# Hybrid encoder block on one core: another order of the head blocks, other PSUM banks for the pooling products, and other start addresses for the out projection's operands

## The chip, the cores and the metric

The kernel runs as one program on one core of a Trainium2 chip. The metric is the device time of one execution in microseconds (us), as the median of several runs. The profiled execution is a separate one with its own time.

## What is computed

One layer of a hybrid encoder block on x of 256 tokens by 1024 channels, all in float32:

```
h = rmsnorm(x) * gain
z = h @ w_in        # 8192 columns: a_in 512 | a_gate 512 | q, k, v 1536 each | b_gate 512 | merge gates 2048
y_a = (per-group linear(multi-scale centred mean pooling(a_in) - a_in) * scale * silu(a_gate)) @ w_proj_a
att = dilated attention(q, k, v) with relative-position bias   # 3 dilation groups x 8 heads of 64
y_b = (att * silu(b_gate)) @ w_proj_b
merge = sigmoid(gA) * y_a + sigmoid(gB) * y_b
y = rmsnorm(x + merge @ w_out) * final_gain
```

## The kernel before

**Precision.** Each product is made of three matmuls in a rounded float32 format (`mm3`, lines 248 to 251). Both operands are split into a high part, a copy in that format (by ScalarE, line 129 for weights), and a low part, the remainder (by VectorE, line 134). The three are high by high, high by low and low by high, summed in PSUM. Every weight tile of 8 KB a partition is loaded by a DMA (line 112) into one of four raw buffers, and then cut into high and low parts, which have three buffers each. `cut_half` does half a tile, and a call of it follows nearly every accumulation tile, so that the cuts run a few tiles ahead of the matmuls.

**Tiles.** A projection tile (`project_t`, `project_v`) is an accumulation of 8 x 3 = 24 matmuls of 128 x 128 by 256 columns into one of three PSUM banks, tag "mm". In `project_t` the weights are stationary and the normalized input's parts `hh` and `hl` are moving; for v (`project_v`) it is the other way round. The other PSUM tags are "S" (one buffer of two banks, for the scores), "T" (two single banks, for transposes) and "O" (one bank, for the attention outputs).

**Order of the work.** The heads are done in two halves I = 0 and 1. The program runs through k, q and v of half 0, then six weight tiles for the pooling input u, its gate a and the attention gate b (two accumulation tiles for each weight tile), then v, k and q of half 1, then the eight weight tiles of the merge gates g (`gate_tile`, sixteen accumulation tiles), with the pooling products mx ahead of the last of them. Then follow the two branch projections y (`branch`: with the pooling branch's AMH and AML, then with the attention's ATHL), and last the out projection (`out_mm`, accumulators "both" and "out"), whose stationary operands are MH and ML, the parts of the merged result; its weights are moving.

**The head blocks.** A half has eight blocks (I, hq, b): four heads and two blocks b of 128 queries. A block has three stages. `stage_s` makes the scores with four matmuls into S (names sp), then VectorE adds the bias (lines 297 and 303, the latter with the row's extreme), ScalarE takes the exponential (306), VectorE divides by the sum (309 to 312). `stage_t` turns three 128 x 128 pieces with PE (line 318, pt) and splits them (320, 321). `stage_o` makes the value products (lines 332 and 335, op) into O, one half of the bank for each b, and after b = 1 the bank is read by ScalarE (346) and twice by VectorE (347, 348).

A small planner, `step()` (lines 355 to 372), puts these stages between accumulation tiles. It is called after each of them. Each call may do one value product, one transpose stage and one score stage, in this order. A transpose stage is due two calls after its scores (`LAG_T`), a value product two calls after the transposes (`LAG_O`). Scores start by a due time: every call with blocks waiting adds `rate`, and when `due` is over 0.99 the next block starts and 1 is taken off. The rate is 0.5 for half 0, where the blocks lie in u, a, b, and v of half 1, and 0.667 for half 1, where they lie in the merge gates. Lines 497 and 560 put the eight blocks of a half into the waiting list.

Outside the opening, the instructions of an engine are ordered by a scheduler which mostly follows the order of the program text; the waits between engines are generated. Buffers with one tag follow each other in turn. The keys are needed on the other 64 partitions too, and are copied there by DMAs from GpSimd's queue (line 442), one for even and one for odd heads of each dilation group.

**Addresses.** SBUF slots are laid out in the order in which their tags first appear. `skip(n, name)` reserves n bytes that nothing uses, so it moves the slots behind it. As built, these are the start addresses modulo 512 bytes: `hh` and `hl` 64, all high and low weight parts 128, AMH, AML and ATHL 64, MH and ML 192. Steps inside these tiles are multiples of 512 bytes. MH lies in the slot "bias", which holds the bias tables BT before, and ML in the slot "kl", 32 elements behind its start.

Of the kernel before, what the change touches and what calls it, by code (L numbers as in the profile page):

```python
# [12 lines left out]
F32R = mybir.dt.float32r  # L13
# [4 lines left out]
P = 128  # L18
D = 1024
S = 256  # L20
# [22 lines left out]
def encoder_block(ctx: ExitStack, tc: tile.TileContext, x, w_in, lines, w_pool, w_proj_a, w_proj_b,  # L43
# [9 lines left out]
    def slot(shape, dt, tag, name, bufs=1):  # L53
        return sb.tile(shape, dt, tag=tag, name=name, bufs=bufs)

    def skip(nbytes, name):

        if nbytes:
            sb.tile([P, nbytes // 4], F32, name=name)

    def bank(shape, tag, name, bufs):
        return ps.tile(shape, F32, tag=tag, name=name, bufs=bufs)

    def mmb(name, shape=(P, S)):
        return bank(list(shape), "mm", name, 3)
# [76 lines left out]
    def weights(n):  # L142
        return parts.pop(n)
# [28 lines left out]
    with tc.manual_schedule(engines={mybir.EngineType.Activation, mybir.EngineType.DVE, mybir.EngineType.PE,  # L172
# [35 lines left out]
        acc = bank([P, 2, 512], "S", "k00", 1)  # L208
# [39 lines left out]
    def mm3(acc, ah, al, bh, bl, first, last):  # L248
        nc.tensor.matmul(acc, ah, bh, start=first, stop=False)  # L249
        nc.tensor.matmul(acc, ah, bl, start=False, stop=False)  # L250
        nc.tensor.matmul(acc, al, bh, start=False, stop=last)  # L251
# [34 lines left out]
    def stage_s(I, hq, b):  # L286
        q = QS[I]
        bs = slice(b * P, (b + 1) * P)
        bl, bt = BL[I], BT[I]

        sp = bank([P, 2 * 512], "S", f"sp{I}{hq}{b}", 1)
        for g in (1, 2):
            o = sp[:, 0:512].rearrange("p (x c) -> p x c", x=2)[:, :, (g - 1) * P:g * P]
            nc.tensor.matmul(o, q[:, hq, g, bs], KX[I][:, hq, g - 1, b], start=True, stop=True)
        for x in range(2):
            nc.tensor.matmul(sp[:, 512:768], q[:, hq, 0, bs], K1[I][:, hq, x], start=x == 0, stop=x == 1)
        nc.vector.tensor_tensor(bl, sp[:, S:2 * S], bt[:, hq, 384:640], op=ALU.add)
        st = slot([P, 512], F32, "st", f"st{I}{hq}{b}", 3)
        nm = slot([P, 1], F32, "nm", f"nm{I}{hq}{b}", 3)
        bias_ = bass.AP(tensor=bl.tensor, offset=bl.offset,  # L300
                        ap=[list(bl.ap[0]), [S + hq * 640 + P * (1 - b), 2], [1, S]])
        scores = bass.AP(tensor=sp.tensor, offset=sp.offset, ap=[list(sp.ap[0]), [512, 2], [1, S]])
        nc.vector.tensor_tensor_reduce(st.rearrange("p (a c) -> p a c", c=256), scores, bias_, scale=-1.0,  # L303
                                       scalar=3.0e38, op0=ALU.add, op1=ALU.min, accum_out=nm)
        l = slot([P, 1], F32, "l", f"l{I}{hq}{b}", 3)
        e = nc.scalar.activation(st, st, AF.Exp, bias=nm, scale=-1.0, accum_out=l)  # L306
        behind(e, last_sig[0])

        nc.vector.tensor_tensor(st[:, P:S], st[:, P:S], st[:, 0:P], op=ALU.add)
        rl = slot([P, 1], F32, "rl", f"rl{I}{hq}{b}", 3)  # L310
        nc.vector.reciprocal(rl, l)
        nc.vector.tensor_scalar(st[:, P:], st[:, P:], rl, None, op0=ALU.mult)
        return st

    def stage_t(I, hq, b, st):
        tp = bank([P, 3, P], "T", f"pt{I}{hq}{b}", 2)
        for c in range(3):
            nc.tensor.transpose(tp[:, c, :], st[:, (c + 1) * P:(c + 2) * P], ident)
        pp = slot([P, 3, 2, P], F32R, "pp", f"pp{I}{hq}{b}", 2)
        nc.scalar.activation(pp[:, :, 0, :], tp, AF.Copy)  # L320
        nc.vector.tensor_tensor(pp[:, :, 1, :], tp, pp[:, :, 0, :].bitcast(F32), op=ALU.subtract)
        return pp
# [3 lines left out]
    def stage_o(I, hq, b, pp):  # L326
        if b == 0:
            opens[I, hq] = bank([P, 2, 2, P], "O", f"op{I}{hq}", 1)
        op = opens[I, hq]
        v = VS[I]  # L330
        for c in range(2):
            nc.tensor.matmul(op[:, b], v[:, c, hq], pp[:, 1 + c], start=c == 0, stop=False)
        for e in range(2):
            q = slice(e * 64, e * 64 + 64)
            nc.tensor.matmul(op[:, b, :, q], v[:, 2 + 2 * b + e, hq], pp[:, 0, :, q], start=False, stop=e == 1)
        if b == 1:
            h = I * 4 + hq
            rows = slice((h % 2) * 64, (h % 2) * 64 + 64)
            dst = ATT[rows, h // 2, :].rearrange("p (b r j) -> p b r j", b=2, r=2)

            def piece(lo, part):
                ap = op[lo * 64:lo * 64 + 64]
                return bass.AP(tensor=ap.tensor, offset=ap.offset + part * P + 63,
                               ap=[list(ap.ap[0]), [2 * P, 2], [64, 2], [-1, 64]])

            last_exp[0] = nc.scalar.activation(dst, piece(0, 0), AF.Copy)
            nc.vector.tensor_tensor(dst, dst, piece(0, 1), op=ALU.add)
            nc.vector.tensor_tensor(dst, dst, piece(1, 0), op=ALU.add)
# [4 lines left out]
    due, rate = [1.0 - RATES[0]], [RATES[0]]  # L353

    def step():
        clock[0] += 1
        for it in live:
            if it["at"] == "t" and it["when"] <= clock[0]:
                stage_o(*it["it"], it["p"])
                it["at"] = "done"  # L360
                break
        live[:] = [it for it in live if it["at"] != "done"]
        for it in live:
            if it["at"] == "s" and it["when"] <= clock[0]:
                it["p"] = stage_t(*it["it"], it["st"])
                it["at"], it["when"] = "t", clock[0] + LAG_O
                break
        due[0] = due[0] + rate[0] if wait else due[0]
        if wait and due[0] > 0.99:
            due[0] -= 1.0  # L370
            it = wait.pop(0)
            live.append({"it": it, "at": "s", "when": clock[0] + LAG_T, "st": stage_s(*it)})
# [95 lines left out]
    def bias(I):  # L468
        T = skew.pop(I)
        t = slot([P, S + 4 * 640], F32, "bias", f"BT{I}")  # L470
        BL[I], BT[I] = t[:, 0:S], t[:, S:].rearrange("p (h c) -> p h c", c=640)
        by = T.rearrange("p c a h -> p h a c")
        for h in range(4):
            nc.gpsimd.tensor_copy(BT[I][:, h, 0:384].rearrange("p (a c) -> p a c", c=64), by[:, h, 0:6])
        for rl in range(2):
            rows = slice(rl * 64, (rl + 1) * 64)
            for g in range(2):
                o = 384 + g * P + 64 * (rl if g == 0 else 1 - rl)
                nc.gpsimd.tensor_copy(BT[I][rows, :, o:o + 64], by[rows, :, 6 + g + rl])
                o = 384 + g * P + 64 * (1 - rl if g == 0 else rl)  # L480
                behind(nc.gpsimd.memset(BT[I][rows, :, o:o + 64], MASK), first_lo)
# [6 lines left out]
    heads(0, "k")  # L488

    heads(0, "q")  # L490
    bias(0)
    U = sb.tile([P, 4, UW], F32, tag="uu", name="U")
    nc.gpsimd.memset(U[:, :, 0:PAD], 0.0)
    nc.gpsimd.memset(U[:, :, PAD + S:], 0.0)
    heads(0, "v")
    skip(608, "pt")
    wait += [(0, hq, b) for hq in range(4) for b in range(2)]


    for dst in ("u", "a", "b"):  # L500
        for t in range(2):
            hi, lo = weights(n)
            for u in range(2):
                acc = project_t(hi, lo, u, f"{dst}{t}{u}")
                g = 2 * t + u
# [50 lines left out]
    heads(1, "q")  # L556
    bias(1)
    rate[0] = RATES[1]
    due[0] = 1.0 - rate[0]
    wait += [(1, hq, b) for hq in range(4) for b in range(2)]  # L560


# [25 lines left out]
    PH, PL = PHL[:, 0], PHL[:, 1]  # L588
# [6 lines left out]
    AML = slot([P, 4, S], F32R, "t4", "AML")  # L595
    wph, wpl = weights(n)
    n += 1
    for g in range(4):
        acc = mmb(f"mx{g}") if g < 3 else bank([P, 2, 512], "S", "mx3", 1)[:, 0, 0:S]
        mm3(acc, wph[:, g, :], wpl[:, g, :], PH[:, g, :], PL[:, g, :], True, True)  # L600
        am = AM[:, g, :].rearrange("p (r j) -> p r j", r=4)
        nc.vector.scalar_tensor_tensor(am, acc.rearrange("p (j r) -> p r j", r=4), prm[:, 24 + g:25 + g],
                                       SA[:, g, :].rearrange("p (r j) -> p r j", r=4), op0=ALU.mult,
                                       op1=ALU.mult)
# [47 lines left out]
    squash((GG[:, 8:12], G2))  # L652

    MH = slot([P, 8, S], F32R, "bias", "MH")
    ML = slot([P, 8 * S + 32], F32R, "kl", "ML")[:, 32:].rearrange("p (c j) -> p c j", j=S)

    def done_b(cb, acc):
        nc.vector.tensor_tensor(GB[cb], acc, GB[cb], op=ALU.mult)
        nc.gpsimd.tensor_tensor(GA[:, cb, :], GA[:, cb, :], GB[cb], op=ALU.add)
        nc.scalar.activation(MH[:, cb, :], GA[:, cb, :], AF.Copy)  # L660
        nc.vector.tensor_tensor(ML[:, cb, :], GA[:, cb, :], MH[:, cb, :].bitcast(F32), op=ALU.subtract)

# [22 lines left out]
    def out_mm(kh, nh, tb):  # L685
        hi, lo = wo[kh, nh]
        c = slice(tb * P, (tb + 1) * P)
        for i in range(2):
# [4 lines left out]
            for k in range(4):  # L693
                kc = kh * 4 + k
                mm3(acc, MH[:, kc, c], ML[:, kc, c], hi[:, k, cs], lo[:, k, cs], kc == 0, kc == KC - 1)

# [145 lines left out]
```

## Time and profile before

| | |
|---|---|
| median of 3 runs | 260.26 us (259.99 to 260.36) |
| profiled execution | 260.05 us, span 258.3 us |
| mean granted TensorE clock | 0.993 |
| matmuls / weight loads | 2160 / 2160 |
| DMA | 52.01 MB in 9992 packets |

The page of the profile lists the engines' busy time, the chain of work that ended last, and the costliest groups of instructions by line. The timeline lists instructions by start and length, with the idle time of the engine before them and what ended it. The windows view sums each engine's busy time in a stretch; there "(x147)" counts the instructions that touch the stretch. Durations of matmuls overlap, since the next one starts before the last has left the array, so the distance between starts, not the duration, is what one costs. PE stands for the matmuls, PEld for the weight loads, DVE for VectorE, ACT for ScalarE, POOL for GpSimd.

### The profile page before, as it was taken

Reading aid. Unit: us, or ns where it says so; the run is one execution under the profiler, and the core shown is the slowest. Engines: PE = TensorE matmul, PEld = TensorE weight load, DVE = VectorE, ACT = ScalarE, POOL = GpSimd, SP = SyncE. Lnnn points to the kernel's source line nnn. Section 1 sums busy time; section 2 is a strip of 40 time slices with the busy share of each in tenths; the row PEclk is TensorE's granted clock in tenths of the full one; section 3 lists DMA queues with packets and bytes.
Section 4 is the critical chain, followed back from the end, with each engine's and each line's share of the span. In section 5 each row is a group of like instructions: output and inputs, shape, how many; then the busy total and the mean of one; then the engine's idle time right before and its main releaser. Section 6 shows DMA issues by size and latency. Waiting matters only on the chain.

```text
span 258.3 us, 5483 instructions
## 1 busy us (share of the span) xinstructions
PE 250.5 (97%) x2160; PEld 249.1 (96%) x2160; DVE 209.4 (81%) x408; ACT 164.6 (64%) x286; POOL 76.6 (30%) x105
## 2 busy tenths in 40 slices
PE   8999999999999999999999999999999999999990
PEld 8899999999999999999999999999999999999990
DVE  2899979778888787889697997967849998899383
ACT  4878577565666565658967778655549994446140
POOL 1562419201798000010671950000210030442011
PEclk9999999999999999999999999999999999999997
DMA  6998999996444644454899897144440598300022
GB/s 232 385 414 325 275 258 326 302 323 241 166 162 162 246 162 166 162 165 162 261 259 210 287 249 302 46 165 162 160 167 0 179 371 291 141 3 1 3 81 81
DMA packets 9992, 52.01 MB, mean 201 GB/s; under 512 B 1147, under 2 KB 2142, under 8 KB 4718
## 3 DMA queue, kind: packets, MB, share of 16 engines
q1 hardware_dynamic: 7022, 44.08, 49.6%
q0 software_dynamic: 2512, 7.12, 11.2%
q10 hardware_dynamic: 432, 0.46, 0.5%
q8 instruction: 17, 0.28, 0.4%
q14 instruction: 9, 0.07, 0.1%
HBM read 47.42 MB, written 1.09 MB: 188 GB/s over the span
## 4 chain that ended last, share of the span: by engine, by line
PE 86%; DVE 6%; issue 3%; DMA 2%; ACT 1%; POOLq 0%; POOL 0%; SPq 0%; DVEq 0%; ACTq 0%
PE v L249 4%; PE v L251 4%; PE v L250 4%; PE q L251 4%; PE q L249 4%; PE q L250 4%; PE g L249 4%; PE g L251 4%; PE g L250 4%; PE k L249 4%; PE k L251 4%; PE k L250 4%; PE y L249 3%; PE y L251 3%; PE y L250 3%
## 5 line engine op out<-in xcount | busy, mean ns | idle before, releaser
L134 DVE TENSOR_TENSOR wlo<-wraw,whi 128x512 fp32r<-128x512 f32 (+1 forms) x130 | 107.5, 865 | 8.3 <-ACT whi L129 7.4
L129 ACT ACTIVATE whi<-wraw 128x1024 fp32r<-128x1024 f32 (+1 forms) x80 | 81.0, 1038 | 22.7 <-PE q L250 10.1
L249 PE MATMUL g<-hh,whi 128*128 128x256 f32 x128 | 35.8, 279 | 0.0
L251 PE MATMUL g<-hh,wlo 128*128 128x256 f32 x128 | 35.4, 276 | 0.0
L250 PE MATMUL g<-hl,whi 128*128 128x256 f32 x128 | 35.3, 276 | 0.0
L306 ACT ACTIVATE st<-st,nm 128x512 f32<-128x512 f32 x16 | 11.6, 724 | 28.7 <-DVE nm L303 28.7
L249 PE MATMUL v<-whi,hh 128*128 128x256 f32 x96 | 26.6, 277 | 0.0
L251 PE MATMUL v<-whi,hl 128*128 128x256 f32 x96 | 26.5, 276 | 0.0
L250 PE MATMUL v<-wlo,hh 128*128 128x256 f32 x96 | 26.5, 276 | 0.0
L251 PE MATMUL q<-hh,wlo 128*128 128x256 f32 x96 | 26.5, 276 | 0.0
L249 PE MATMUL q<-hh,whi 128*128 128x256 f32 x96 | 26.5, 276 | 0.0
L250 PE MATMUL q<-hl,whi 128*128 128x256 f32 x96 | 26.5, 276 | 0.0
L249 PEld LDWEIGHTS g<-hh,whi 128*128 128x128 f32 x128 | 24.0, 188 | 0.1
L250 PEld LDWEIGHTS g<-hl,whi 128*128 128x128 f32 x128 | 24.0, 188 | 0.0
L251 PEld LDWEIGHTS g<-hh,wlo 128*128 128x128 f32 x128 | 24.0, 188 | 0.0
L249 PE MATMUL k<-hh,whi 128*128 128x256 f32 x80 | 22.2, 277 | 0.0
L251 PE MATMUL k<-hh,wlo 128*128 128x256 f32 x80 | 22.1, 277 | 0.0
L250 PE MATMUL k<-hl,whi 128*128 128x256 f32 x80 | 22.1, 277 | 0.0
L250 PEld LDWEIGHTS v<-wlo,hh 128*128 128x128 f32 x96 | 18.0, 188 | 0.0
L250 PEld LDWEIGHTS q<-hl,whi 128*128 128x128 f32 x96 | 18.0, 188 | 0.0
L251 PEld LDWEIGHTS q<-hh,wlo 128*128 128x128 f32 x96 | 18.0, 188 | 0.0
L249 PEld LDWEIGHTS q<-hh,whi 128*128 128x128 f32 x96 | 18.0, 188 | 0.0
(179 smaller groups left out, 764.1 us busy)
## 6 DMA issues: line engine op xcount, KB each, us to landing
wraw<-in_w_in_dram SPq DMA_DIRECT2D x31, 1024.0 KB, 6.6
wraw<-in_w_out_dram SPq DMA_DIRECT2D x4, 1024.0 KB, 5.6
T<-line_d POOLq DMA_DIRECT2D x4, 576.0 KB, 8.7
KX<-KX POOLq DMA_DIRECT2D x8, 256.0 KB, 17.2
wraw<-in_w_proj_a_dram SPq DMA_DIRECT2D x2, 1024.0 KB, 4.9
wraw<-in_w_proj_b_dram SPq DMA_DIRECT2D x2, 1024.0 KB, 4.9
X<-in_x_dram SPq DMA_DIRECT2D x2, 512.0 KB, 4.2
wraw<-in_w_in_dram SPq DMA_DIRECT2D x2, 512.0 KB, 6.6
```

Source lines behind the costliest of these rows:

```text
L129: nc.scalar.activation(hi[:, s, :], t[:, s, :], AF.Copy)
L134: (nc.gpsimd if kind == "pool" else nc.vector).tensor_tensor(lo[:, s, :], t[:, s, :], hi[:, s, :].bitcast(F32), op=ALU.subtract)
L249: nc.tensor.matmul(acc, ah, bh, start=first, stop=False)
L250: nc.tensor.matmul(acc, ah, bl, start=False, stop=False)
L251: nc.tensor.matmul(acc, al, bh, start=False, stop=last)
L306: e = nc.scalar.activation(st, st, AF.Exp, bias=nm, scale=-1.0, accum_out=l)
```

## The change

There are four edits, none of which changes a value that is computed.

1. A call of `step()` stands between v and u of half 0. The first block's scores come there, and all later stages of half 0 one accumulation tile earlier.
2. The due time at the start of half 1 is 2 x (1 - 0.667) = 0.666 in place of 0.333, so the blocks' scores follow other calls of `step()`.
3. The first two pooling products keep the "mm" banks and the third and fourth get the two banks of S; before, three had "mm" banks and the fourth the first bank of S. All twelve matmuls are written ahead of the four readings by VectorE.
4. Of the 608 bytes left empty behind the slot "bias", 384 are moved ahead of it, and ML starts at its slot's beginning. So MH moves by +384 bytes and ML by -128; both then start at 64 modulo 512. Slots further behind stay where they were.

```diff
--- before.py
+++ after.py
@@ -488,13 +488,16 @@
     heads(0, "k")
 
     heads(0, "q")
+    skip(384, "pb")
     bias(0)
     U = sb.tile([P, 4, UW], F32, tag="uu", name="U")
     nc.gpsimd.memset(U[:, :, 0:PAD], 0.0)
     nc.gpsimd.memset(U[:, :, PAD + S:], 0.0)
     heads(0, "v")
-    skip(608, "pt")
+    skip(224, "pt")
     wait += [(0, hq, b) for hq in range(4) for b in range(2)]
+
+    step()
 
 
     for dst in ("u", "a", "b"):
@@ -556,7 +559,8 @@
     heads(1, "q")
     bias(1)
     rate[0] = RATES[1]
-    due[0] = 1.0 - rate[0]
+
+    due[0] = 2.0 * (1.0 - rate[0])
     wait += [(1, hq, b) for hq in range(4) for b in range(2)]
 
 
@@ -595,9 +599,13 @@
     AML = slot([P, 4, S], F32R, "t4", "AML")
     wph, wpl = weights(n)
     n += 1
+
+    pair = bank([P, 2, 512], "S", "mx2", 1)
+    mx = [mmb("mx0"), mmb("mx1"), pair[:, 0, 0:S], pair[:, 1, 0:S]]
     for g in range(4):
-        acc = mmb(f"mx{g}") if g < 3 else bank([P, 2, 512], "S", "mx3", 1)[:, 0, 0:S]
-        mm3(acc, wph[:, g, :], wpl[:, g, :], PH[:, g, :], PL[:, g, :], True, True)
+        mm3(mx[g], wph[:, g, :], wpl[:, g, :], PH[:, g, :], PL[:, g, :], True, True)
+    for g in range(4):
+        acc = mx[g]
         am = AM[:, g, :].rearrange("p (r j) -> p r j", r=4)
         nc.vector.scalar_tensor_tensor(am, acc.rearrange("p (j r) -> p r j", r=4), prm[:, 24 + g:25 + g],
                                        SA[:, g, :].rearrange("p (r j) -> p r j", r=4), op0=ALU.mult,
@@ -652,7 +660,7 @@
     squash((GG[:, 8:12], G2))
 
     MH = slot([P, 8, S], F32R, "bias", "MH")
-    ML = slot([P, 8 * S + 32], F32R, "kl", "ML")[:, 32:].rearrange("p (c j) -> p c j", j=S)
+    ML = slot([P, 8 * S + 32], F32R, "kl", "ML")[:, 0:8 * S].rearrange("p (c j) -> p c j", j=S)
 
     def done_b(cb, acc):
         nc.vector.tensor_tensor(GB[cb], acc, GB[cb], op=ALU.mult)
```

## Prediction

> **What bounds the kernel now.** I read the page first, for the busy shares and the chain that ended last.
>
> ```profile
> PE 250.5 (97%) x2160; PEld 249.1 (96%) x2160; DVE 209.4 (81%) x408; ACT 164.6 (64%) x286; POOL 76.6 (30%) x105
> PE 86%; DVE 6%; issue 3%; DMA 2%; ACT 1%; POOLq 0%; POOL 0%; SPq 0%; DVEq 0%; ACTq 0%
> ```
>
> The matmul stream fills the span: 2160 matmuls, and the chain lies on PE for 86%. So time can come from two places only: holes in that stream, and the distance between two matmuls that follow each other without a hole. The windows view shows the second. A row gives the stretch, its length, the busy time and count of PE, the weight loads, DVE, ACT and POOL, and last the granted clock, the DMA share and GB/s. The stretches here begin at a tile's first matmul and hold whole tiles of 24 matmuls; each count has 3 matmuls more that were still running at the stretch's start.
>
> ```profile
> 26.88:43.20 16.32, 16.32 (x147) 16.32 (x145) 14.16 (x19) 10.93 (x18) 7.25 (x9) 1.00 1.07 285
> 43.20:59.52 16.32, 16.32 (x147) 16.32 (x145) 12.81 (x23) 9.83 (x16) 3.56 (x4) 1.00 1.11 314
> 59.52:62.35 2.83, 2.83 (x27) 2.83 (x25) 1.76 (x5) 2.62 (x4) 0.00 (x0) 1.00 0.95 304
> 75.93:81.59 5.66, 5.66 (x51) 5.66 (x49) 4.71 (x11) 3.20 (x6) 5.20 (x9) 1.00 0.52 185
> 115.62:121.35 5.73, 5.73 (x51) 5.73 (x50) 5.48 (x8) 4.91 (x9) 0.00 (x0) 1.00 0.37 114
> 229.37:249.16 19.79, 19.79 (x171) 19.79 (x170) 14.80 (x33) 7.20 (x15) 3.68 (x4) 1.00 0.01 2
> ```
>
> The first row is q, the second v: 144 matmuls in 16.32 us, 113.3 ns each. The last is seven tiles of the out projection: 168 matmuls of the same shape in 19.79 us, 117.8 ns each. The granted clock is 1.00 in both, PE is never idle in either, and the DMA share is 0.01 in the slow one, so neither clock, waits nor transfers make the 4.5 ns. The wide spacing is also in u's first tile (2.83 us for 24: 117.9 ns) and in two pairs of tiles at 75.93 and 115.62. It begins at some upset of the stream, stays until the next one, and costs 24 x 4.5 ns = 0.11 us a tile.
>
> Then the timeline of PE, for holes. It has two clusters. The first stands in the gate stage, ahead of a value product (op):
>
> ```profile
> 188.26 0.28 PE L251 MATMUL g<-hh,wlo 128*128 128x256 f32 x1
> 188.71 0.47 PE L332 MATMUL op<-pp,VS 128*128 128x256 f32 x2 [0.17 <-DVE ATT L348]
> ...
> 189.46 0.37 PE L249 MATMUL g<-hh,whi 128*128 128x256 f32 x1
> 189.67 0.28 PE L250 MATMUL g<-hl,whi 128*128 128x256 f32 x1
> ...
> 198.99 0.39 PE L332 MATMUL op<-pp,VS 128*128 128x256 f32 x2
> ```
>
> From 188.26 to 188.71 are 0.45 us where 0.11 is usual, and the pair of op then takes 0.47 where the undisturbed one at 198.99 takes 0.39. That is 0.34 + 0.08 = 0.42 us. The releaser is VectorE's last addition out of the single O bank:
>
> ```profile
> 188.13 0.42 DVE L348 TENSOR_TENSOR ATT<-ATT,op 64x256 f32<-64x256 f32 x1
> ```
>
> The second cluster stands in the four pooling products (mx):
>
> ```profile
> 200.32 0.28 PE L251 MATMUL mx<-PHL,wlo 128*128 128x256 f32 x1
> 200.55 0.38 PE L249 MATMUL mx<-PHL,whi 128*128 128x256 f32 x1
> 200.77 0.28 PE L250 MATMUL mx<-PHL,whi 128*128 128x256 f32 x1
> ...
> 201.24 0.28 PE L251 MATMUL mx<-PHL,wlo 128*128 128x256 f32 x1
> 201.44 0.38 PE L249 MATMUL g<-hh,whi 128*128 128x256 f32 x1
> 201.66 0.28 PE L250 MATMUL g<-hl,whi 128*128 128x256 f32 x1
> ```
>
> Four distances of 0.23, 0.22, 0.20 and 0.22 us stand where 0.113 is usual: 0.87 - 0.45 = 0.42 us. What they wait for is a buffer of the three mm banks:
>
> ```profile
> 200.04 0.46 ACT L574 ACTIVATE G<-g,prm 128x256 f32<-128x256 f32 x1
> ...
> 200.90 0.48 DVE L602 SCALAR_TENSOR_TENSOR SA<-mx,prm,SA 128x256 f32<-128x256 f32 x1
> ```
>
> The third product starts at 200.55, right behind ScalarE's reading of the last gate accumulator (to 200.50). The gate tile behind the products starts at 201.44, right behind VectorE's reading of the first product (to 201.38).
>
> **The head blocks in groups** (due 0.666 in place of 0.333). With a rate of 0.667 the scores of the eight blocks fell after gate steps 1, 3, 4, 6, 7, 9, 10, 12; now they fall after 1, 2, 4, 5, 7, 8, 10, 11. A block's transposes come two steps later, its value products four. Both halves of a head share the O bank, which is free once the second half is read. Second halves fell on steps 7, 10, 13 and the next head's first half on 8, 11, 14: one step for the reading. Now they are 6, 9, 12 and 8, 11, 14: two steps. VectorE ended that reading at 188.55, a whole step of over 2.7 us before the new need, so the 0.42 us goes. What is late next is the S bank: scores of step 2 now follow those of step 1 directly, and need VectorE's reading (L303) of the first.
>
> ```profile
> 156.89 0.68 DVE L303 CUSTOM_DVE_ANT_1 st<-sp,BT 128x512 f32<-128x512 f32 x1
> ```
> ```profile
> 157.65 0.28 PE L249 MATMUL g<-hh,whi 128*128 128x256 f32 x1
> ```
>
> It ended at 157.57 and step 2 is at 157.65, a margin of 0.08 us. The cost is 0 if VectorE's order stays, and up to 0.6 if one more piece of that 0.68 us size goes ahead; I take 0.1, being nearest the row. The later neighbours (4-5, 7-8, 10-11) repeat what 6-7 and 9-10 were before. Steps with a break of the gate stream were 14 and are now 15; one break costs about the 0.21 - 0.11 = 0.10 us seen at 189.46. So this part: -0.42 + 0.1 + 0.1 = -0.22 us.
>
> **The pooling products in the double bank.** Products three and four get the two halves of S, which the last scores left at step 11. They no longer wait for the gate reading. The gate tile behind takes the bank that the last gate accumulator left at 200.50, no longer the first product's. Without the first two distances it would start near 201.1, so 0.6 us of cover remain; if ScalarE reads later than that, the cost is the lateness. That the twelve matmuls are now written ahead of VectorE's four readings changes no order on either queue. I take the whole: -0.42 us.
>
> **First scores between v and u.** All eight blocks of the first half move up one tile. The wide spacing of u lasted three tiles, up to the first transposes, and those now come after two. I expect the wide state to begin in the scores, as it began at v's end before, so one tile is gained: -0.11 us. At both ends: +0.1 if a later break falls into it for one tile more, -0.33 if the scores shield u. What the move can make late is, first, the copies of the keys to the other partitions, issued on POOL's queue:
>
> ```profile
> 30.61 1.30 POOL L442 DMA_DIRECT2D KX<-KX  x2 [2.80 <-DVE KX L430]
> ```
> ```profile
> DMA to landing us min/median/max: 23.8/27.1/28.9
> ```
>
> The first block is an even head and needs the earlier of this last pair: 30.61 + 27.1 = 57.7, at the worst 59.5, against v's end at 59.52. Cost 0 now; it grows one for one if the copy lands later. Second, the transposes, which now stand after u's second tile:
>
> ```profile
> 60.52 0.86 DVE L400 TENSOR_TENSOR VS<-v,VS 64x256 fp32r<-64x256 f32 x2 [0.97 <-ACT VS L398]
> 61.47 1.89 DVE L134 TENSOR_TENSOR wlo<-wraw,whi 128x512 fp32r<-128x512 f32 x3
> 63.39 0.42 DVE L297 TENSOR_TENSOR BT<-sp,BT 128x256 f32<-128x256 f32 x1
> ...
> 66.63 0.42 DVE L312 TENSOR_SCALAR st<-st,rl 128x384 f32<-128x384 f32 x1
> ```
> ```profile
> 68.47 0.49 PE L318 MATMUL pt<-ident,st 128*128 128x128 f32 x3
> ```
>
> The probabilities were ready at 67.05, 1.4 us before their transposes and 4.7 us after the scores' start at 62.35. The same 4.7 us from 59.52 end at 64.2; the transposes come near 59.52 + 0.47 + 2 x 2.83 = 65.65. But VectorE's first step (L297) came 1.04 us after that start, and now v's evacuation holds it back to 61.38, 1.86 us after: the chain ends near 65.0, and 0.6 us of cover remain. One weight cut more in front (0.63 us by the row of three) uses it up, and each further one would cost 0.6 us; I take 0.
>
> **The operands' phase.** In the built program the normalized input's parts (hh, hl) start 64 bytes past a multiple of 512, the weight parts 128, ATHL 64, and MH and ML 192. The change moves MH by 384 bytes and ML by -128, so both stand at 64. Then the out projection has to the byte (in 512) the phases of v: stationary at 64, moving at 128, entered from a tile whose moving operand stands at 64, as v is entered from q. That v runs at 113.3 ns in the second windows row. So 192 matmuls x 4.5 ns = 0.86 us at the most; nothing at the least; and I take 0.86, since the nearest row is v's. Against it speaks the row at 115.62, where a v tile with those very phases is wide after an upset.
>
> The Trainium skill, "TensorE: Matmul & The Clock Gate", section "Back-to-back issue gap", gives a distance that depends on the moving length alone, and its "Step-by-step" says that loading weights takes no read bandwidth from the running matmul. By it the phase is worth 0; the rows disagree so far that 113.3 and 117.8 ns stand side by side at one length and one clock.
>
> Whether the gain reaches the end is seen in the last rows of VectorE:
>
> ```profile
> 235.49 4.31 DVE L134 TENSOR_TENSOR wlo<-wraw,whi 128x512 fp32r<-128x512 f32 x7
> 243.70 0.76 DVE L708 TENSOR_TENSOR XL<-both,XL 128x256 f32<-128x256 f32 x2 [3.91 <-PE both L251]
> ...
> 252.18 0.42 DVE L708 TENSOR_TENSOR XL<-out,XL 128x256 f32<-128x256 f32 x1 [0.16 <-PE out L251]
> ```
>
> VectorE has cut the last weights at 239.80 and sits idle 3.91 us for PE; the last addition waits for PE too. With 0.86 us less that cover is not used up.
>
> **The sum.** -0.22 - 0.42 - 0.11 - 0.86 = -1.6 us. The profiled execution took 260.05 us (span 258.3 and 1.75 around it), 0.21 below the median of 260.26. So 258.4 for such an execution and 258.65 by the median; I say 258.5.
>
> **Rivals.**
> *The phase does nothing.* What holds the wide state is the upset at the projection's start, not the address. For it: the wide pair at 115.62. Against it: the v row, and that q, at other phases, is narrow as well, so both states exist and v's entry found the narrow one. The time is 258.5 + 0.86 = 259.3. The Trainium skill's page "TensorE: Matmul & The Clock Gate" would give the same by the rule named above.
> *The lags come back.* VectorE is late from 172 to 188, and the waits taken away reappear at the scores or transposes that follow, and in the pooling products' successors. For it: the margin of 0.08 us at step 2. Against it: the new order has the same neighbours later on. 260.05 - 0.86 - 0.11 + 0.2 = 259.3; if the phase fails too, 260.1.
> *Slower: the wide spacing catches the gate stage.* It is narrow today, though broken 14 times; if step 2's early scores put it into the wide state and no later break frees it, 16 gate tiles pay 0.11 us each, 1.8 us. It outweighs the rest from 15 tiles on if the phase gives its gain, from 7 if not; in the latter case the time is 259.3 + 1.8 = 261.1. Against it: every transpose in the first half but two led back to the narrow state.
>
> **Chances.** The forecast 0.58, the phase nothing 0.22, the lags back 0.08, both failing 0.06, slower 0.06. A measurement can tell about 0.2% (0.5 us) from no change here. Faster by more takes the first three, less a little for costs added: 0.84; within 0.09; slower 0.07. The range runs from 260.05 - 1.6 - 0.2 (the two taken costs gone) - 0.4 (the four other wide tiles freed) = 257.8 to the phase rival with the S bank's 0.6: 259.9.
>
> **What would show it.** Right: the out projection's seven tiles in 19.04 us instead of 19.79, matmuls of 276 ns and not 281; no distance over 0.21 us ahead of op in the gate stage; the twelve mx matmuls at 0.113 with one break at most ahead of them; the first transposes after two tiles of u. Wrong: any new hole with a releaser at sp of gate step 2 or at the first pt, or wide spacing in the gate tiles or still in the out projection.

## The result and the profile after

| | before | after |
|---|---|---|
| median | 259.98 us (259.85 to 260.36, 6 runs) | 266.27 us (265.24 to 267.07, 6 runs) |
| profiled execution | 260.05 us, span 258.3 | 266.37 us, span 264.6 |
| mean granted TensorE clock | 0.993 | 0.986 |

The changed kernel is slower: the ratio is 1.0234, 95% interval 1.0218 to 1.025. In all comparisons here, runs more than 1.5% above the fastest of the same kernel are left out; where a kernel's own times fall into two groups, I give the groups or the single times.

The first reading is the same two lines of the page: busy shares, and the chain that ended last.

```profile
PE 252.9 (96%) x2160; PEld 251.2 (95%) x2160; DVE 211.5 (80%) x408; ACT 165.3 (62%) x286; POOL 72.8 (28%) x105
PE 86%; issue 5%; DVE 4%; DMA 2%; ACT 1%; POOLq 0%; POOL 0%; SPq 0%; DVEq 0%
```

The work is the same, 2160 matmuls. PE is busy 2.4 us longer and the span is 6.3 us longer, so about 4 us are holes and the rest is matmuls that follow each other more slowly. Where, is read from the starts of each stretch's first matmul (k' and q' are those of half 1):

| stretch | before | after | difference |
|---|---|---|---|
| start to first v of half 0 | 43.20 | 43.02 | -0.18 |
| v to first k' (v, head blocks of half 0, v of half 1) | 75.33 | 77.14 | +1.81 |
| k' to first q' | 16.91 | 19.94 | +3.03 |
| q' to first g | 16.32 | 18.04 | +1.72 |
| g to mx | 47.90 | 47.84 | -0.06 |
| mx to y | 7.72 | 7.33 | -0.39 |
| y to the out projection | 21.99 | 22.37 | +0.38 |
| out projection | 22.50 | 22.50 | 0.00 |

The sum is +6.31 us. (One value product moves from the third stretch to the second, 0.41 us.) The list of PE's waits and PE's timeline name the largest piece:

```profile
PE q L249 <- DVE KX L430: 3.0, 1, 3.0
```
```profile
136.79 0.28 PE L251 MATMUL k<-hh,wlo 128*128 128x256 f32 x1
140.10 0.36 PE L249 MATMUL q<-hh,whi 128*128 128x256 f32 x1 [3.03 <-DVE KX L430]
```

From 136.79 to 140.10 are 3.31 us where 0.12 is usual: a hole of 3.19 us. The q tile needs a bank whose key VectorE has not read yet. VectorE's timeline says why, and GpSimd's what ran beside it:

```profile
131.07 1.23 DVE L134 TENSOR_TENSOR wlo<-wraw,whi 128x1024 fp32r<-128x1024 f32 x1
132.32 0.86 DVE L430 TENSOR_TENSOR KX<-k,KX 64x256 fp32r<-64x256 f32 x2
133.21 5.84 DVE L134 TENSOR_TENSOR wlo<-wraw,whi 128x1024 fp32r<-128x1024 f32 x1
139.08 0.88 DVE L430 TENSOR_TENSOR KX<-k,KX 64x256 fp32r<-64x256 f32 x2
139.99 1.23 DVE L134 TENSOR_TENSOR wlo<-wraw,whi 128x1024 fp32r<-128x1024 f32 x1
```
```profile
132.22 1.31 POOL L555 TENSOR_TENSOR SB<-SB,sgsb 128x512 f32<-128x512 f32 x1
133.45 3.37 POOL L474 COPY BT<-T 128x384 f32<-128x384 f32 x4
136.77 3.36 POOL L479 COPY BT<-T 64x256 f32<-64x256 f32 x4
```

One weight cut takes 5.84 us, its neighbours of the same shape 1.23. During it GpSimd makes the bias copies of half 1 without a pause, and the key readings queue behind the cut. The seventh copy, taken by itself, says when VectorE got its turn:

```profile
138.00 1.55 POOL L479 COPY BT<-T 64x256 f32<-64x256 f32 x1
```

It takes 1.55 us where the two before it take 0.62 each, and the sixth ended at 137.96, 1.09 us before the cut ends. By these spans the cut was shut out for six copies, and the seventh then waited for the cut. In the kernel before, those copies came 7 us later, since the second table load was issued only at 132.10 and waited for:

```profile
122.22 0.53 POOL L466 DMA_DIRECT2D T<-line_d  x1 [7.88 <-PE op L335]
...
132.10 0.59 POOL L466 DMA_DIRECT2D T<-line_d  x1
133.98 1.29 POOL L442 DMA_DIRECT2D KX<-KX  x2 [1.30 <-DVE KX L430]
140.91 3.87 POOL L474 COPY BT<-T 128x384 f32<-128x384 f32 x4 [5.64 <-DMA T<-line_d]
```

After the change both loads stand together ahead of the sigmoid products. They go into the buffer that v of half 0 had, which the last value product (PE op) sets free:

```profile
120.62 1.03 POOL L466 DMA_DIRECT2D T<-line_d  x2 [7.98 <-PE op L335]
```

The windows view of the changed kernel (columns as before) gives the stretch with the hole, the q tile behind it, and the last seven tiles:

```profile
134.09:140.10 6.01, 2.98 (x26) 2.81 (x25) 5.92 (x4) 3.68 (x7) 5.97 (x9) 1.00 0.63 199
140.10:144.54 4.44, 4.44 (x25) 4.44 (x25) 4.30 (x6) 0.00 (x0) 2.65 (x5) 0.62 0.72 167
235.68:255.47 19.79, 19.79 (x171) 19.79 (x170) 14.81 (x33) 7.16 (x15) 3.69 (x4) 1.00 0.01 2
```

Behind the hole the granted clock falls: mean 0.62 over the q tile, which takes 4.44 us instead of 2.72; 15 of its matmuls start 213 ns apart. That is the +1.72 of the next stretch. The last row answers the prediction's first test: the seven out tiles take 19.79 us, as before, and not 19.04.

Half 0 lost the rest. The first transposes, for which the prediction worked out 0.6 us of cover, did come after two tiles of u and without a wait (65.47; the probabilities ended at 64.90). The wait is at the third block:

```profile
78.81 0.34 PE L335 MATMUL op<-pp,VS 128*128 128x128 f32 x2
79.67 0.52 PE L318 MATMUL pt<-ident,st 128*128 128x128 f32 x3 [0.52 <-DVE st L312]
```
```profile
75.23 1.83 DVE L134 TENSOR_TENSOR wlo<-wraw,whi 128x512 fp32r<-128x512 f32 x2
76.98 0.72 DVE L309 TENSOR_TENSOR st<-st 128x128 f32<-128x128 f32 x1
77.63 0.15 DVE L311 RECIPROCAL rl<-l 128x1 f32<-128x1 f32 x1
77.70 1.12 DVE L134 TENSOR_TENSOR wlo<-wraw,whi 128x512 fp32r<-128x512 f32 x1
78.74 0.78 DVE L312 TENSOR_SCALAR st<-st,rl 128x384 f32<-128x384 f32 x1
```
```profile
77.63 2.48 POOL L529 TENSOR_TENSOR win<-win 128x269 f32<-128x269 f32 x3
```

The op matmul is followed 0.79 us later by the transpose, where 0.11 is usual. Between the row's extreme and the division (L312) stand three half cuts. The first runs while ScalarE takes the exponential; the other two lie in the block's chain, and everything is stretched beside GpSimd's window additions. In the kernel before, the division of the same block is stretched beside these additions too, but no cut stands ahead of it:

```profile
79.28 0.35 DVE L309 TENSOR_TENSOR st<-st 128x128 f32<-128x128 f32 x1 [0.88 <-ACT st L306]
79.55 0.15 DVE L311 RECIPROCAL rl<-l 128x1 f32<-128x1 f32 x1
79.74 0.79 DVE L312 TENSOR_SCALAR st<-st,rl 128x384 f32<-128x384 f32 x1
```

From the extreme to the end of the division this chain took 2.1 us before and takes 4.2 now. This wait and two smaller ones (0.12 at 99.8, 0.17 at 113.7) make 0.96 us; five more wide tiles in v of half 1 make 0.55, two in k' with their two breaks 0.25, and one less wide in u saves 0.11.

Two steps did what they should. The pooling products run without a wait, and op in the gate stage too:

```profile
206.38 0.28 PE L249 MATMUL mx<-PHL,whi 128*128 128x256 f32 x1
206.50 0.28 PE L250 MATMUL mx<-PHL,whi 128*128 128x256 f32 x1
206.62 0.28 PE L251 MATMUL mx<-PHL,wlo 128*128 128x256 f32 x1
206.73 0.28 PE L249 MATMUL mx<-PHL,whi 128*128 128x256 f32 x1
```
```profile
195.27 0.28 PE L251 MATMUL g<-hh,wlo 128*128 128x256 f32 x1
195.38 0.39 PE L332 MATMUL op<-pp,VS 128*128 128x256 f32 x2
```

### The profile page after: what moved, and what is told of

Its sections match the earlier page's. It is cut to its first block, busy times and chain, and to the rows that moved or that the text cites. A ratio compares the mean times of both kernels' runs of the same rounds, so it can differ in the third digit from the quotient of the medians.

```text
span 264.6 us, 5494 instructions
## 1 busy us (share of the span) xinstructions
PE 252.9 (96%) x2160; PEld 251.2 (95%) x2160; DVE 211.5 (80%) x408; ACT 165.3 (62%) x286; POOL 72.8 (28%) x105
## 3 DMA queue, kind: packets, MB, share of 16 engines
HBM read 47.42 MB, written 1.09 MB: 183 GB/s over the span
## 4 chain that ended last, share of the span: by engine, by line
PE 86%; issue 5%; DVE 4%; DMA 2%; ACT 1%; POOLq 0%; POOL 0%; SPq 0%; DVEq 0%
PE g L249 6%; PE g L251 6%; PE g L250 6%; PE q L249 4%; PE q L250 4%; PE q L251 4%; PE v L249 4%; PE v L250 4%; PE v L251 4%; PE y L249 3%; PE k L249 3%; PE y L250 3%; PE y L251 3%; PE k L250 3%; PE k L251 3%
## 5 line engine op out<-in xcount | busy, mean ns | idle before, releaser
L134 DVE TENSOR_TENSOR wlo<-wraw,whi 128x512 fp32r<-128x512 f32 (+1 forms) x130 | 111.9, 886 | 18.8 <-ACT whi L129 17.8
L129 ACT ACTIVATE whi<-wraw 128x1024 fp32r<-128x1024 f32 (+1 forms) x80 | 81.9, 1039 | 34.4 <-PE q L250 10.3
L249 PE MATMUL q<-hh,whi 128*128 128x256 f32 x96 | 27.4, 285 | 3.0 <-DVE KX L430 3.0
L250 PE MATMUL q<-hl,whi 128*128 128x256 f32 x96 | 27.2, 284 | 0.0
L251 PE MATMUL q<-hh,wlo 128*128 128x256 f32 x96 | 27.2, 283 | 0.0
L249 PEld LDWEIGHTS q<-hh,whi 128*128 128x128 f32 x96 | 18.7, 195 | 3.2 <-ACT whi L129 3.2
L250 PEld LDWEIGHTS q<-hl,whi 128*128 128x128 f32 x96 | 18.8, 196 | 0.0
L251 PEld LDWEIGHTS q<-hh,wlo 128*128 128x128 f32 x96 | 18.8, 196 | 0.0
L249 PEld LDWEIGHTS v<-whi,hh 128*128 128x128 f32 x96 | 18.0, 188 | 0.0
```

The source lines that it names most:

```text
L129: nc.scalar.activation(hi[:, s, :], t[:, s, :], AF.Copy)
L134: (nc.gpsimd if kind == "pool" else nc.vector).tensor_tensor(lo[:, s, :], t[:, s, :], hi[:, s, :].bitcast(F32), op=ALU.subtract)
```

## Experiments

Three theories were set against each other for the loss. P: GpSimd's copies and VectorE's cut shut each other out. R1: the loss has nothing to do with the moved scores. R2: what hurts is that the table loads land earlier, as transfers. For the phase there are A (it does nothing) and B (it sets out's spacing).

**Which edit loses: the score step alone, and everything but it**

```diff
+    step()                      # before, with this line alone, between v and u
```

> The kernel before with the first edit alone, the call of step() between v and u. Theory P: that call lets both loads of the second bias table go out together once the last value product of half 0 is done, GpSimd's bias copies then run in one piece from about 133 us, and VectorE's weight cut (two SBUF inputs) is held back as long (5.84 us in place of 1.23 in the changed kernel), with the key evacuations queued behind it. Then the hole of 3.2 us between k and q and the half clock behind it (1.7 us) are here too, with the 1.4 us lost in half 0, and none of the gate stage's gain of 0.45: 266 to 267 us. Rival R1: the hole comes of the other edits (due time, banks, addresses): then 260 to 261.5 us and no hole between k and q.

Measured: 266.41, 261.49, 265.03 and 265.84 us, median 265.43 (before: 259.97 to 260.03 beside all experiments). The profiled execution (266.41) has the same picture: a cut of 5.83 us at 133.03 beside the eight copies, a wait of 3.0 us ahead of q, half the clock behind it. One line makes the loss; R1 falls. One of the four runs (261.49) escaped most of it.

> The changed kernel without the first edit: due time, pooling banks and addresses alone. Theory P: no hole between k and q, GpSimd's bias copies again from about 141 us in two pieces; the gate stage gives its 0.4 to 0.6 us and the out projection nothing: 259.3 to 259.7 us. If the addresses work once the stream comes in undisturbed, 258.5. Rival R1: 264 to 265.5 us, with the hole.

Measured: 259.07 us (258.82 to 260.32, 12 runs), ratio 0.9972 (0.9961 to 0.9984). No hole between k and q. Nine runs lie near 259.0 and three at 260.0 to 260.3. The profiled one is of the three: y gets new waits and falls into the wide spacing from its third tile to the end. Of the nine no trace exists.

**The phase alone**

```diff
+    skip(384, "pb")
-    skip(608, "pt")
+    skip(224, "pt")
-    ML = ...[:, 32:]...
+    ML = ...[:, 0:8 * S]...
```

> The kernel before with the fourth edit alone: MH moved by 384 bytes, ML by -128. Theory A, the phase does nothing and the wide spacing of the out projection is held by the upset ahead of it: 259.8 to 260.2 us, out tiles of 2.83 us. Theory B, the phase decides and only the wide state at the end of y spoilt it in the changed kernel: 259.0 to 259.3 us, out tiles of 2.72 us.

Measured: 259.30 us (259.08 to 260.0 in six runs; two more took 265.96 and 361.64 at mean granted clocks of 0.948 and 0.658), ratio 0.9975 (0.9964 to 0.9985). The windows view of its last seven tiles:

```profile
229.45:248.50 19.05, 19.05 (x171) 19.05 (x170) 14.69 (x33) 7.20 (x15) 3.69 (x4) 1.00 0.01 2
```

19.05 us was forecast as 19.04. A falls for this kernel; the out projection is 0.84 us shorter.

**The copies later, or on another engine**

```diff
+            if I:
+                behind(e, last_dup[0])   # half 1's bias copies after the last key copy on GpSimd
```

> The changed kernel with the second half's bias copies ordered on GpSimd behind the last copy of the keys, so that they start at about 140 us and not at 133; nothing else is moved by hand. Theory P: VectorE's cut at 133 takes about 1.2 us, at most some 2 us against the gating products, the hole of 3.2 us and the half clock are gone: 266.3 - 4.9 = 261.4, within 260.8 to 262 us. Rival R2: the hole comes of transfers (the bias tables' loads, early and together, delay the weights): then it stays and the time is 265 to 267 us.

Measured: 261.55 us (261.36 to 262.69), ratio 1.0069 (1.0053 to 1.0085). The loads still go out early (120.61); the copies moved to 141.62, and the hole and the half clock are gone. R2 falls. That the time is so near the forecast is in part luck. Between the profiled executions (266.37 and 261.38) only 4.3 of the 5.0 us come from k' and q': the q tiles, no longer broken by the hole, stay wide at 2.83 us. Another 0.85 come from the out projection, which is narrow here (28.06 us from its first matmul to the end instead of 28.91).

```diff
-            nc.gpsimd.tensor_copy(...)
+            nc.scalar.activation(..., AF.Copy)    # for half 1
```

> The changed kernel with the twelve bias copies of the second half on ScalarE instead of GpSimd, everything else as it is. Theory P (a VectorE operation with two SBUF inputs and the GpSimd copies shut each other out): nothing is left on GpSimd beside the weight cut at 133.2, the cut takes about 1.2 us and not 5.84, the 3.0 us wait between k and q and the half clock behind it go, and the time is 266.3 less 4.7, so 261.0 to 262.2. Rival R (it is VectorE's own order, or the transfers that land earlier, whoever copies): the wait stays, 265 to 267. In both the losses of the first half stay (the first transposes 0.7 us late, the wide spacing).

Measured: 264.09 us (263.25 to 264.7), ratio 1.0158 (1.0142 to 1.0174): between the two forecasts. The cuts are normal (two in 2.36 us), as P says, but the copies now hold up ScalarE's half of the key reading:

```profile
131.88 4.01 ACT L476 ACTIVATE BT<-T 128x384 f32<-128x384 f32 x5
...
136.58 0.77 ACT L428 ACTIVATE KX<-k 64x256 fp32r<-64x256 f32 x2
```

PE waits for the key twice, 1.8 us together. I had not asked what queues behind the copies on their new engine.

**How long the lockout lasts: smaller cuts, and one copy more**

```diff
-        m = (k + 1) // 2 if 9 <= n <= 18 or n >= 24 else k
+        m = (k + 1) // 2 if n >= 9 else k
```

> The changed kernel with the weight cuts of k and q of the second half in pieces of 256 elements instead of 512. It asks how long VectorE is shut out: if GpSimd keeps the other side through a whole run of back-to-back copies, each piece that meets the run is held as long as the whole was, and the time stays at 264 to 267. If VectorE gets in between two copies, a piece loses one copy at the most (3.4 us, four copies, less what it had done), key reads queued behind come earlier, and the time falls to 261 to 263.5. The changed lengths alone cost VectorE about 0.1 us a cut, which is not on the path there.

Measured: 261.69 us (260.57 to 261.8), ratio 1.0056 (1.0039 to 1.0073). No hole; VectorE got in between the copies:

```profile
134.44 0.88 DVE L430 TENSOR_TENSOR KX<-k,KX 64x256 fp32r<-64x256 f32 x2
135.35 2.51 DVE L134 TENSOR_TENSOR wlo<-wraw,whi 128x512 fp32r<-128x512 f32 x2
137.87 0.42 DVE L430 TENSOR_TENSOR KX<-k,KX 64x256 fp32r<-64x256 f32 x1
```

```diff
+        if I:
+            nc.gpsimd.tensor_copy(BT[I][:, 0, 0:64], by[:, 0, 0])    # a short copy ahead of the eight
```

> The changed kernel with one short extra GpSimd copy (128x64) ahead of the bias copies of the second half; its result is overwritten by the copy behind it. GpSimd's copies start where they did, the full ones about 0.2 us later. Theory T (whether VectorE gets its turn between two copies hangs on how the two queues meet, so a shift of a few tenths of a us can free it): the weight cut takes 1.5 to 3 us and not 5.84, the hole between k and q shrinks or goes, 261.5 to 264. Rival L (once a run of copies has begun, VectorE's cut of 1024 elements is shut out to its end): the cut takes 5.8 to 6.1 us, and the time is 266.3 to 266.6.

Measured: 266.66, 266.81, 264.89 and 261.13 us. In the profiled execution (266.66) the cut takes 6.06 us: 0.22 more for a copy of 0.30.

```diff
+        if I:
+            nc.gpsimd.tensor_copy(BT[I][:, 0, 0:384]..., by[:, 0, 0:6])    # the first copy twice
```

> The changed kernel with the first bias copy of the second half (128x384) made twice. Nine copies in a row instead of eight. Rival L (shut out to the end of the run): the cut takes 0.9 us more, 6.7 us, the hole grows by as much, and the time is about 267.2. Theory T (it hangs on how the queues meet; the same first copy starts at the same time): the cut is as long as before or shorter, at most 266.5.

Measured: 266.86, 267.45, 261.87 and 268.3 us. The profiled execution (266.86):

```profile
133.30 6.64 DVE L134 TENSOR_TENSOR wlo<-wraw,whi 128x1024 fp32r<-128x1024 f32 x1
```

That is 0.80 us more for one copy more (0.84 each in a row of four, 3.37 us). In this trace seven copies stand in a row and two follow only at 142.03. In all four traces of the lockout (the changed kernel, the score step alone and these two) the cut ends 1.09 us behind the second of the 64x256 copies, so after six, six, seven and seven copies. Once shut out, VectorE's cut waits nearly to the end of the series, close to what rival L says, and a copy added ahead adds about its own length. But in three of these kernels (all but the changed one) one run of four came out near 261 to 262 us; no profile exists of such a run, so that VectorE gets its turn there is likely but not shown.

**Early tables without the moved step**

```diff
+    bias_load(1)        # ahead of the sigmoids, in the kernel with both phase and banks
     for t_, nm_ in ((SA, "sa"), (SB, "sb")):
...
-    bias_load(1)
```

> The kernel before with the pooling products in the double bank and the phase (258.73), and the load of the second half's bias tables written ahead of the gates' sigmoids. No step is moved. The tables then land earlier, and the GpSimd copies fall beside the weight cuts and key reads at about 134 to 142 us. Theory P: a VectorE cut of over 3 us appears there, k or q waits, and the time rises by 1 to 4 us, to 259.7 to 263. If the hole needs the lags that the moved step gives the first half, nothing happens: 258.7 to 259.0.

Measured: 258.67 to 258.94 in three runs and 259.68 to 260.26 in seven; the profiled one of the seven has no wait for a key and a wide out projection. P's forecast of a cut over 3 us and a wait failed. GpSimd's queue put the copies at 137.72, not at 133. The cut began beside the last sigmoid product (136.50 to 137.77) and got in ahead of the first copy, which took 1.88 us instead of 0.89:

```profile
136.61 2.25 DVE L134 TENSOR_TENSOR wlo<-wraw,whi 128x1024 fp32r<-128x1024 f32 x1 [0.40 <-ACT whi L129]
```
```profile
137.72 5.40 POOL L474 COPY BT<-T 128x384 f32<-128x384 f32 x4
```

So the neighbourhood is needed (copies later, or elsewhere: no lockout), but does not always bring it. What decides whether VectorE is let in at the first copy or only after six stays open.

**The waits of half 0**

```diff
+            behind(e, last_exp[0])     # window additions, asked to stand behind the head blocks' exponentials
```

> The changed kernel with the late bias copies (261.55), and in addition the GpSimd window additions of the pooling branch held back behind the head blocks of u, a and b; VectorE's order is the same. It asks what makes the transposes of the third block wait 0.7 us at 79.7. If GpSimd's additions beside VectorE's cuts do it (the two cuts there take 1.83 and one 1.12 where 1.29 and 0.67 are usual): cuts at the usual time, no wait there, 260.7 to 261.0 (a new wait where the additions now fall may give some of it back). If the two cuts that stand between the row's extreme and the division in VectorE's order do it alone, the wait stays at 0.5 or more, 261.4 to 261.7.

Measured: 261.9 us (261.17 to 262.65), ratio 1.0075 (1.0058 to 1.0092). The additions did not move away, they were only reordered among themselves at 64 to 84 us. The wait at 79 went and others came (0.18 at 72.4, 0.41 at 86.1). The time lies above both forecasts. The third block's chain, with the same three cuts but its additions moved by some 1 to 2 us, took 3.4 us instead of 4.2. So the run does not separate the two causes: the cuts are new against the kernel before, and where the additions meet the chain it is longer.

**The gate stage's edits with the phase**

```diff
-    due[0] = 1.0 - rate[0]
+    due[0] = 2.0 * (1.0 - rate[0])
```

> The kernel before with two parts: the operands' phase and the head blocks in groups (due 0.666). Against the phase alone (259.30): if the O bank's 0.42 us is a real gain that reaches the end, 258.8 to 259.0. If what is gained in the gate stage is given back in the y stage (as in the run of three parts, where the y tiles had new stalls of 0.45 us) or by the wait for the S bank at step 2 (0.15 us), 259.2 to 259.6.

Measured: 259.32 us (nine runs at 259.12 to 259.38, three at 259.99 to 260.53), ratio 0.9983 (0.9973 to 0.9993). The profiled run (259.99) is of the three, with y's last tile and the out projection wide. In it the O bank's wait is gone, but the pooling products then wait 0.41 us (526 ns instead of 113 ahead of the third) for ScalarE's gate reading: nothing is left against the phase alone (259.30).

```diff
+    pair = bank([P, 2, 512], "S", "mx2", 1)
+    mx = [mmb("mx0"), mmb("mx1"), pair[:, 0, 0:S], pair[:, 1, 0:S]]    # as in the change
```

> The kernel before with two parts: the operands' phase and the pooling products in the double bank. If the pooling waits (0.35 to 0.42 us) go and nothing takes their place, 258.9 to 259.0, and the out projection stays at 2.72 us a tile. If the earlier products bring the y tiles' stalls (VectorE and ScalarE late in the squash), 259.3 to 259.7, with y and out at 2.83 us a tile.

Measured: 258.73 us (258.68 to 258.89, 5 runs), ratio 0.9955 (0.9943 to 0.9967): the best version, faster than both kernels. From mx to y 7.29 us instead of 7.72, and y gives back 0.09. Its out projection:

```profile
228.88:247.93 19.05, 19.05 (x171) 19.05 (x170) 14.69 (x33) 7.21 (x15) 3.70 (x4) 1.00 0.01 2
```

> The kernel before with the phase and the pooling banks once more (258.73 in five runs). The run with the early tables has the same y and out code and gave 258.67 to 258.94 in three runs and 259.68 to 260.26 in seven, with out wide in the profiled one. If the narrow spacing at out's entry is a matter of chance in each run, some runs here too are at 259.7 to 260.3; if this kernel's timing at the end of y always leaves the narrow one, all are at 258.6 to 258.9.

Measured: 258.92 us (258.75 to 260.03, 6 runs), ratio 0.9965 (0.9951 to 0.9978). Five of six stay below 259.3 and one does not; of both runs together ten of eleven. So, judged by the times, it is a matter of chance in each run, with the odds on the narrow side here. The median of all eleven is 258.78.

**The phase in a second kernel, and half of it**

> The kernel before with the pooling products in the double bank and the old operands' phase. It is the run of both parts (258.73) without the phase. Theory B (which spacing the out projection gets is set by the phase of MH and ML against the tile before, as long as that tile ends narrow): out's tiles at 2.83 us, first distances 114, 119, 117, and 258.73 + 0.7 to 0.8 = 259.5. Rival (the spacing follows from how the last wait in y happens to end, and the two runs with narrow out were luck): out narrow here too, 258.7 to 258.9, or times spread between both.

Measured: 259.58 us (259.25 to 259.82, 11 runs), ratio 0.9982 (0.9974 to 0.9991). y ends narrow as in the best version, and out is wide:

```profile
228.97:248.75 19.78, 19.78 (x170) 19.78 (x169) 14.79 (x33) 7.20 (x15) 3.68 (x4) 1.00 0.01 2
```

Against the same kernel with the phase, the phase is worth 0.85 us in the median of its first five runs and 0.80 in that of all eleven. Theory B holds here too. All traces together say the same. With MH at 64, the out projection kept the spacing in which y's last tile ended: narrow in six traces, wide in eight. With MH at 192 it was wide in all three (the kernel before, the score step alone, this one), though y ended narrow in each. No other start of MH was tried.

> The kernel before with the pooling products in the double bank and MH alone moved to 64 modulo 512; ML stays at 192. ML is the stationary operand of one matmul of three. If all three matmuls' phases count, the wide spacing returns, 259.4 to 259.5. If the entry is set by the first matmuls, whose operand is MH, out stays narrow, 258.7. If only the matmuls with ML are wide, out's tiles take about 2.76 us and the time is 259.0.

Measured: eight runs at 258.67 to 258.87 and four at 260.11 to 260.5. By their times the eight have the narrow spacing, so MH alone seems enough in most runs, but no trace of one of them exists. The profiled run (260.11) is one of the four: a wait in y's third tile leaves the wide spacing, and it is kept through five more y tiles into out, at about 2.85 us a tile.

## Why the prediction was wrong

**First scores between v and u: the step that failed.** It was costed at -0.11 us; alone it costs 5.4 us in the median (265.43 against 260.03), and on top of the other three edits 7.2 (266.27 against 259.07). The two covers that I worked out held: no wait for the key copies, none at the first transposes. What failed is the list of "what the move can make late". I stopped at the first block. All eight blocks move, so the last value product ends a tile earlier and frees the buffer of the table loads earlier; in the scheduler's order both loads then stand ahead of GpSimd's sigmoid products, and the copies behind them fall beside the weight cut at 133 instead of after the keys at 141. I had neither read the row of these copies in the old place nor asked who runs beside them in the new one. The hole of 3.19 us and the q tile at a clock of 0.62 (1.72 us) follow from that, shown by the copies moved later (261.55): without the lockout both are gone.

The second part is 1.4 us in half 0. Of it 0.68 us is the wait at the third block, the danger that I named ("each further one would cost 0.6 us") and then took at 0; I had worked out the cover for the first block only. The rows point to the cuts ahead of the division, but that they do it without GpSimd's additions is not shown. The rest is two smaller waits (0.29) and five wide tiles in v of half 1 (0.55), for which I had allowed +0.1. The forecast -0.11 in u did come.

The Trainium skill, "SBUF — State Buffer", section "SBUF: two separate sides", says that a VectorE operation with two SBUF inputs and a GpSimd operation that reads SBUF exclude each other for a whole instruction. The cut and the copies are such a pair and the trace agrees that one blocks the other; the other way round, the seventh copy waits for the cut (1.55 us instead of 0.62). But 5.84 us are not one instruction's wait, they hold six copies', so the measurement goes beyond the rule.

**The slower rival** had the wrong mechanism: it put the wide spacing into the gate tiles (1.8 us), and these gained 0.06 us.

**Head blocks in groups: the mechanism right, the sum too good.** The O bank's 0.42 us went. The S bank's wait at step 2 came, as feared at 0.1: 174 and 192 ns where about 113 stood, 0.14 us. The breaks of the gate stream cost 0.14 more and one wide gate tile 0.10, which by this count leaves about -0.04; the stretch from g to mx measures -0.07, where -0.22 was forecast. With the phase alone beside it (259.32), the next stretch, mx to y, gives even that back.

**Pooling products in the double bank: right.** -0.39 us of the forecast -0.42 in the changed kernel, and -0.43 with the phase. The cover for the gate tile behind held.

**The operands' phase: right where the projection is entered narrow, without effect in the profiled run here.** 0.84 and 0.86 us against the forecast 0.86, in two kernels. In the changed kernel's profiled run the last y tile ends wide after a wait, and matching phases keep the state, whichever it is. It need not end so: in the profiled runs of three variants of the changed kernel (copies late, additions late, first copy twice) it ends narrow, and the out projection is narrow. How such a wait ends stays open. The prediction saw that against it spoke "the row at 115.62, where a v tile with those very phases is wide after an upset" and did not carry it over: y has such an upset halfway through its last tile in most traces here.

**What y gives back.** The prediction had no term for y. It takes 0.38 us more here, in new waits in its second and third tile (up to 0.11 us each) and a wide end. With only one of the two edits ahead of it, the groups or the banks (each with the phase), y takes 21.94 or 22.08 us, against 21.99 before and 22.37 here. So it pays when both gains come together; that it then meets VectorE and ScalarE too early is argued, not shown.

**The whole.** Of the forecast -1.6, the three edits without the scores bring -0.96 in the median (259.07; the one profiled run, 260.23, has none of it), and the one line of the scores costs several times that.

## What to carry to other kernels

When a step moves, follow it to its last effect, not its first: which buffer comes free earlier at its end, which load that releases, and on which engine the work behind the load then runs beside what. Two operations that exclude each other should be kept apart by an order of one's own, not by when a load happens to land. A gain that hangs on a state kept from one stage to the next has to be followed back to the last wait ahead of it, and told with the share of runs that have it.

## What the hardware showed that I had not expected

- VectorE can be shut out by a series of GpSimd copies for six or seven of them in a row: 5.84 us for a cut of 1.23, 6.64 with one copy more. Halved cuts were not (two in 2.51 us), nor was a full cut that met the first copy later (2.25 us).
- The same program then falls into two groups of times: 266.86, 267.45, 261.87 and 268.3 us for one kernel.
- A hole of 3.2 us is followed by matmuls at half the clock (213 ns apart, mean 0.62 over the q tile); the hole's true price is 4.9 us. In the four traces with holes of 3.2 to 4.0 us the clock fell so for 3.4 us each time; behind the hole of 1.4 us in the run with ScalarE's copies it stayed at 1.00.
- Matmuls of one shape at a clock of 1.00 have two spacings, 113.3 and 117.8 ns. A wait can end in either. Into the out projection the state was kept in all 14 traces with MH at 64 modulo 512, where ATHL of the tile before stands too; in the three with MH at 192 it was wide each time. Aligning MH alone was enough in eight runs of twelve, judged by their times.
